# First loads on two DMA queues, in smaller first pieces, and the first norm's squares behind the last input chunk, in a two-layer decoder trunk

## The chip, the cores and the metric

The kernel runs on one core of a Trainium2 chip. The metric is the device time of one execution in microseconds (us). TensorE (PE) multiplies matrices, ScalarE (ACT) and VectorE (DVE) work on rows, GpSimd (POOL) builds masks, and SyncE (SP) issues most DMAs. ScalarE can issue DMAs from its own queue as well. Each engine works through its own queue in order.

## The reference

A sequence of 512 tokens, with 16 learned meta tokens ahead of it, goes through two layers of width 1024. The start of the first layer is what matters here:

```python
h = jnp.concatenate([meta, x], axis=1)
hn = rms_norm(h, norm_mix[0])          # y = x * rsqrt(mean(x*x) + EPS) * g
qkv = hn @ w_qkv                       # 16 heads of 64
h = h + stick_breaking(qkv) @ w_o      # causal, scores q.k
h = h + sq_relu_mlp(rms_norm(h, norm_mlp[0]))
# layer 1: RG-LRU mixer and MLP; then a last rms_norm
```

## The kernel before

The activations stand with features on the partitions: eight chunks of 128 features by 544 columns (the 528 tokens, and the 16 meta tokens a second time). A float32 product is made of three matmuls: every operand is split into a high part and the rest (hi and lo), and hi·hi, hi·lo and lo·hi are summed in PSUM. `split` (L61 to L66) makes the two parts: hi by ScalarE (L63), lo by VectorE (L66). `xs_write` (L143 to L148) does the same for an input chunk, times the gain of the norm, which it reads from the table `vecs`: `xh` (L146) on ScalarE, `xl` (L147) on VectorE. Multiplication by the norm's 1/rms is put off: it is applied where the results leave PSUM.

**The start.** SyncE loads `vecs` (52 KB, L126), and then the loop of L275 to L282 loads, in this order: the first half (four chunks of features) of the first query unit's weights (256 KB, L269), input chunks 0 to 3 (272 KB each, L279), the first half of the first key unit, the second query half, chunks 4 to 7, the second key half. Every piece is split as soon as it has landed. `act.preload_act_table_set` (L273) loads ScalarE's table of functions ahead of it all.

**The first products.** 96 matmuls (tiles `z` as outputs) make the first query and key unit from these pieces. `v_load` then loads two pieces of value weights and splits them to `vhi` and `vlo`; these two tiles take the two buffers of the tag "hs", which hold input chunks 0 to 3 and 4 to 7 until everything that reads these chunks is done, the squares of the norm among them. Four windows of values of 24 matmuls each (`pvs`, tiles `g`) follow; a fifth window needs the PSUM buffer of the first two, which `v_out` (L414, L415) gives back.

**The first norm.** `Norm.add` squares a chunk on ScalarE (`acc` L166 for chunk 0, `sq` L169 for the others) and adds it into `acc` on VectorE (L170). There is one buffer `sq`, so square and sum alternate. The eight calls stand behind the first value window in the program, in a block of priority raised by HP // 4 = 100. `first_norm` sums `acc` over the features by matmuls (tiles `o`), takes the root (L84) and the reciprocals (L177, L343). Only then are queries and keys scaled and written (`qk_out`, `put_q`, `put_k`), the values written (`v_out`), and only then the score matmuls of the first head pair start (tiles `z` in `do_z`, which begin with `ident` times a mask). Behind them come eight head pairs of attention, whose query and key products of the next pair fill TensorE, then the MLPs and the recurrent layer.

**What sets the order.** The program is planned ahead: each engine's queue is filled with the instruction of the smallest place in the program, less its raised priority, among those whose operands are there by the plan. `after(ins, earlier)` keeps an instruction behind others of the same engine in that order; it adds no wait between engines.

Of the kernel before, what the change touches and what calls it, by code (L numbers as in the profile page):

```python
# [18 lines left out]
AF = mybir.ActivationFunctionType  # L19
ALU = mybir.AluOpType  # L20
PSUM = bass.MemoryType.PSUM

P = 128
KC = 8
# [3 lines left out]
HT = T // 2  # L28
TX = T + NM
# [11 lines left out]
HP = 400  # L41
# [4 lines left out]
def tile_hybrid_trunk(ctx: ExitStack, tc: tile.TileContext, h0, vec, wqk, wv, wo,  # L46
                      win, wrg, wig, wout, wup, wdn, out):
    nc = tc.nc
    act, dve, pool, pe = nc.scalar, nc.vector, nc.gpsimd, nc.tensor
# [8 lines left out]
    def f32(ap):  # L58
        return ap.bitcast(F32)

    def split(src, hi, lo, hi_eng=None, lo_eng=None):  # L61
        if hi_eng is None or hi_eng is act:
            act.activation(out=hi, in_=src, func=AF.Copy)  # L63
        else:
            hi_eng.tensor_copy(out=hi, in_=src)
        (lo_eng or dve).tensor_tensor(out=lo, in0=src, in1=f32(hi), op=ALU.subtract)  # L66
# [4 lines left out]
    def after(ins, earlier):  # L71
        for i in earlier:
            tc.add_manual_dep(ins.ins, i.ins.name,
                              mybir.DependencyInfo(mybir.DependencyClass.NoSync, mybir.DependencyReason.DATA),
                              reason="table set order")

    def table(out, in_, func, tset, **kw):
        if runs["set"] != tset:
            runs["before"], runs["now"], runs["set"] = runs["now"], [], tset
            if tset == "natural_log_exp_and_others":  # L80
# [8 lines left out]
    LNEXP, EXP, SIG, SQRT, GELU = ("natural_log_exp_and_others", "exp_and_others", "sigmoid_and_others",  # L89
                                   "sqrt_and_others", "gelu_apprx_tanh_and_others")  # L90
# [32 lines left out]
                mm(outs[i], wlo, cut(xhi, i), False, last and j == n - 1)  # L123

    vecs = const.tile([P, NV], F32, name="vecs")
    nc.sync.dma_start(out=vecs, in_=vec)  # L126


    def slot(i, dtype, name, w=TX):
        return xsp.tile([P, w], dtype, tag=f"x{i}", name=name)  # L130
# [7 lines left out]
    xh = [slot(c, F32R, f"xh{c}") for c in range(KC)]  # L138
    xl = [slot(8 + c, F32R, f"xl{c}") for c in range(KC)]
# [3 lines left out]
    def xs_write(c, h_c, g0, c0=0, c1=T):  # L143
        xh, xl = xs["h"], xs["l"]
        g = vecs[:, g0 + c:g0 + c + 1]
        act.activation(out=xh[c][:, c0:c1], in_=h_c[:, c0:c1], func=AF.Copy, scale=g)  # L146
        dve.scalar_tensor_tensor(out=xl[c][:, c0:c1], in0=h_c[:, c0:c1], scalar=g, in1=f32(xh[c][:, c0:c1]),  # L147
                                 op0=ALU.mult, op1=ALU.subtract)  # L148

    ones = const.tile([P, P], F32, name="ones")  # L150
    dve.memset(ones, -1.0)
# [3 lines left out]
    class Norm:  # L155
# [3 lines left out]
            self.c, self.first = slice(c0, c1), True  # L159
            self.acc = stp.tile([P, TX], F32, tag="acc", name="acc")  # L160

        def add(self, c, h_c, cols=None):
            c = cols or self.c
            if self.first:
                self.first = False
                act.activation(out=self.acc[:, c], in_=h_c[:, c], func=AF.Square)  # L166
            else:
                sq = stp.tile([P, TX], F32, tag="sq", name="sq")
                act.activation(out=sq[:, c], in_=h_c[:, c], func=AF.Square)  # L169
                dve.tensor_tensor(out=self.acc[:, c], in0=self.acc[:, c], in1=sq[:, c], op=ALU.add)  # L170

        def finish(self, ps, cols):
            rstd = stp.tile([P, T], F32, tag="rstd", name="rstd")
# [9 lines left out]
    def h_chunk(c):  # L183
        return hs[c // 4][:, c % 4, :]
# [59 lines left out]
    def attention_layer():  # L244
# [5 lines left out]
        def gtile():  # L250
            return gps.tile([P, S], F32, tag="g", name="g")
# [9 lines left out]
        for m in (0, KC):  # L261
            raw = wp.tile([P, KC * P], F32, tag="raw", name="raw", bufs=3)
            w_first.append((m, raw, wp.tile([P, KC * P], F32R, tag="whi", name="whi"),
                            wp.tile([P, KC * P], F32R, tag="wlo", name="wlo")))

        def first_half(i, a, lo_eng=None):
            m, raw, hi, lo = w_first[i]
            half = slice(a * 4 * P, (a + 1) * 4 * P)
            nc.sync.dma_start(out=raw[:, half], in_=wqk[m][:, half])  # L269
            split(raw[:, half], hi[:, half], lo[:, half], None, lo_eng)  # L270

        nrm = Norm(0, TX)
        act.preload_act_table_set(SQRT)  # L273

        for c in range(KC):  # L275
            if c % 4 == 0:
                hs[c // 4] = hsp.tile([P, 4, TX], F32, tag="hs", name="hs")
                first_half(0, c // 4)
            nc.sync.dma_start(out=h_chunk(c), in_=h0[:, c, :])  # L279
            xs_write(c, h_chunk(c), V_MIX0, 0, TX)  # L280
            if c % 4 == 3:
                first_half(1, c // 4)  # L282

# [120 lines left out]
        def v_mm(pv, w, vhi, vlo):  # L404
            for k in range(KC):
                mm(pv, window(xh[k], w), vhi[:, k, :], k == 0, False)
                mm(pv, window(xl[k], w), vhi[:, k, :], False, False)
                mm(pv, window(xh[k], w), vlo[:, k, :], False, k == KC - 1)
# [158 lines left out]
        for w in range(4):  # L567
            if w % 2 == 0:
                gt = gtile()
            pvs.append(gt[:, 256 * (w % 2):256 * (w % 2) + 256])  # L570
            v_mm(pvs[w], w, *vw)
            if w == 0:
                with tc.high_priority(HP // 4):
                    for c in range(KC):
                        nrm.add(c, h_chunk(c))
        with tc.high_priority(1000):
            first_norm()
        with tc.high_priority(HP):
# [39 lines left out]
        for m in range(KC):  # L618
# [4 lines left out]
            for c0, n in ALL:  # L623
                g = gtile()
# [9 lines left out]
        nrm = Norm()  # L634
# [347 lines left out]
    with ExitStack() as ctx_a:  # L982
        nrm, blocks = attention_layer()
# [17 lines left out]
    nrm, blocks = mixer(nrm1, *xm, gtile)  # L1001
# [118 lines left out]
```

## Time and profile before

| | us |
|---|---|
| median of 3 runs | 1194.46 |
| lowest, highest run | 1193.98, 1195.98 |
| the profiled execution, its own time | 1195.73 |
| its span, first to last instruction | 1194.0 |
| TensorE busy | 1166.0 |

All rows below are of the profiled execution, and their times count from the start of its span; 1.73 us lie around it. A row of a timeline merges equal instructions that follow each other and gives their count as x. A matmul's busy time overlaps with the next one's, so the pace of matmuls is read from counts in a stretch. PEclk is the granted TensorE clock as a share of full speed (1.00 is 2.4 GHz, 0.50 is 1.2 GHz).

### The profile page before, as it was taken

The page shows a single profiled execution, that of the slowest core. Times are in us where ns is not written, and L with a number is a line of the kernel's source. Part 1 is how long each engine was busy: PE and PEld are TensorE (multiplying, and loading weights), DVE is VectorE, ACT ScalarE, POOL GpSimd, SP SyncE. Part 2 cuts the span into 40 slices and gives each one's busy share as a digit, 9 for nine tenths or more (in the row PEclk, how much of TensorE's full clock was granted, in tenths as well). Part 3 has the DMA queues.
Part 4 walks back from the last instruction along what each step waited for, and adds up shares of the span by engine and source line. Part 5 has one row for each costly group of instructions (what it writes and reads, how often), then busy time and mean ns, then how long its engine had stood idle before and what let it go on. Part 6 is the DMA issues. An engine that isn't in the chain of part 4 may idle for free.

```text
span 1194.0 us, 20446 instructions
## 1 busy us (share of the span) xinstructions
PE 1166.0 (98%) x8366; PEld 1104.4 (92%) x8366; DVE 875.5 (73%) x1517; ACT 641.3 (54%) x1063; POOL 4.8 (0%) x24
## 2 busy tenths in 40 slices
PE   7999999999899999999999999999999999999997
PEld 7999999999899999999999999878988988988986
DVE  7887778997895585585586677788975865856854
ACT  6776788776673244243244448757642443533542
POOL 1000000000000000000000000000000000000000
PEclk9999999999999999999999999999999999999999
DMA  6321212041122322322322422223323223223322
GB/s 222 102 74 59 85 37 91 19 145 53 57 93 76 113 91 87 110 92 91 109 93 85 130 72 71 73 86 106 102 76 118 95 96 117 90 88 127 103 71 71
DMA packets 33068, 109.69 MB, mean 92 GB/s; under 512 B 3792, under 2 KB 5840, under 8 KB 32976
## 3 DMA queue, kind: packets, MB, share of 16 engines
q1 hardware_dynamic: 32432, 107.87, 27.9%
q8 instruction: 65, 1.06, 0.4%
q10 hardware_dynamic: 544, 0.52, 0.1%
q14 instruction: 27, 0.22, 0.1%
HBM read 101.96 MB, written 2.10 MB: 87 GB/s over the span
## 4 chain that ended last, share of the span: by engine, by line
PE 87%; DVE 7%; ACT 3%; issue 1%; DMA 1%; SPq 0%; DVEq 0%; ACTq 0%
PE g L103 77%; PE z L103 8%; PE o L103 2%; ACT whi L63 1%; DVE wlo L66 1%; DVE acc L170 1%; DVE th L924 0%; DVE xt L66 0%; DVE xl L147 0%; ACT L84 0%; DVE th L961 0%; DMA hs<-in_h_dram 0%; DVE yl L66 0%; DMA raw<-in_wqk_dram 0%; DMA raw<-in_wup_dram 0%
## 5 line engine op out<-in xcount | busy, mean ns | idle before, releaser
L63 ACT ACTIVATE whi<-raw 128x1024 fp32r<-128x1024 f32 (+1 forms) x150 | 155.8, 1044 | 244.8 <-PE g L103 230.0
L103 PE MATMUL g<-hh,whi 128*128 128x264 f32 (+2 forms) x784 | 231.9, 319 | 3.6 <-ACT whi L63 3.5
L103 PE MATMUL g<-hl,whi 128*128 128x264 f32 (+2 forms) x784 | 231.9, 317 | 0.0
L66 DVE TENSOR_TENSOR wlo<-raw,whi 128x1024 fp32r<-128x1024 f32 (+1 forms) x150 | 180.3, 1207 | 23.5 <-ACT whi L63 23.3
L103 PE MATMUL g<-xt,o 128*128 128x256 f32 (+1 forms) x896 | 163.9, 282 | 0.0
L103 PEld LDWEIGHTS g<-hh,whi 128*128 128x128 f32 x784 | 147.6, 189 | 16.6 <-ACT whi L63 6.4
L103 PEld LDWEIGHTS g<-hl,whi 128*128 128x128 f32 x784 | 147.5, 188 | 9.5
L103 PE MATMUL g<-hh,wlo 128*128 128x264 f32 (+2 forms) x784 | 156.1, 318 | 0.0
L103 PEld LDWEIGHTS g<-xt,o 128*128 128x128 f32 x896 | 137.8, 188 | 0.4
L103 PEld LDWEIGHTS g<-hh,wlo 128*128 128x128 f32 x784 | 120.5, 188 | 10.1
L785 DVE TENSOR_TENSOR hs<-g,hs 128x528 f32<-128x528 f32 (+1 forms) x62 | 42.5, 696 | 113.8 <-PE g L103 113.6
L103 PE MATMUL g<-xb,whi 128*128 128x264 f32 (+1 forms) x352 | 65.2, 286 | 3.4 <-DVE u L725 1.9
L103 PE MATMUL g<-xm,whi 128*128 128x264 f32 (+1 forms) x384 | 67.0, 321 | 0.0
L103 PE MATMUL g<-xt,o1l 128*128 128x256 f32 (+1 forms) x224 | 63.3, 283 | 0.0
L84 ACT ACTIVATE sp<-sp 128x272 f32<-128x272 f32 (+3 forms) x128 | 62.4, 511 | 1.6
L103 PE MATMUL g<-xt,o2l 128*128 128x256 f32 (+1 forms) x224 | 62.2, 282 | 0.0
L103 PEld LDWEIGHTS g<-xm,whi 128*128 128x128 f32 x384 | 56.6, 188 | 5.3
L103 PE MATMUL g<-xh,whi 128*128 128x264 f32 x224 | 59.3, 287 | 0.5 <-DVE v L415 0.5
L103 PE MATMUL g<-xl,whi 128*128 128x264 f32 x224 | 59.2, 287 | 0.0
L747 ACT ACTIVATE hh<-t 128x512 fp32r<-128x512 f32 (+1 forms) x56 | 34.8, 632 | 45.1 <-DVE t L738 45.1
L103 PEld LDWEIGHTS g<-xb,whi 128*128 128x128 f32 x352 | 53.3, 188 | 5.0 <-DVE u L725 3.0
L103 PE MATMUL g<-xa,whi 128*128 128x264 f32 (+1 forms) x288 | 52.3, 282 | 0.0
(244 smaller groups left out, 2730.7 us busy)
## 6 DMA issues: line engine op xcount, KB each, us to landing
raw<-in_wup_dram SPq DMA_DIRECT2D x64, 512.0 KB, 3.5
raw<-in_wdn_dram SPq DMA_DIRECT2D x64, 512.0 KB, 3.5
raw<-in_win_dram SPq DMA_DIRECT2D x16, 512.0 KB, 3.4
raw<-in_wqk_dram SPq DMA_DIRECT2D x14, 512.0 KB, 3.6
q<-q SPq DMA_DIRECT2D x16, 264.0 KB, 4.5
raw<-in_wv_dram SPq DMA_DIRECT2D x8, 512.0 KB, 3.5
raw<-in_wo_dram SPq DMA_DIRECT2D x8, 512.0 KB, 3.7
raw<-in_wout_dram SPq DMA_DIRECT2D x8, 512.0 KB, 3.4
```

The costliest lines, as they stand in the source:

```text
L63: act.activation(out=hi, in_=src, func=AF.Copy)
L66: (lo_eng or dve).tensor_tensor(out=lo, in0=src, in1=f32(hi), op=ALU.subtract)
L84: ins = act.activation(out=out, in_=in_, func=func, **kw)
L103: return pe.matmul(out=o, lhsT=lhsT, rhs=rhs, start=start, stop=stop, skip_group_check=True)
L170: dve.tensor_tensor(out=self.acc[:, c], in0=self.acc[:, c], in1=sq[:, c], op=ALU.add)
L747: act.activation(out=h_, in_=x, func=AF.Square)
L785: dve.tensor_tensor(out=h3, in0=g[:, 0:nb, 0:cw], in1=h3, op=ALU.add)
```

## The change

`vecs` and the first half of the first query unit are issued by ScalarE's queue instead of SyncE's; that half comes in two pieces (one chunk of features, 64 KB, and three, 192 KB), each split by itself. Input chunk 0 comes in two pieces of columns (264 and 280), each with its own `xh` and `xl`. The table load stands behind the first half's instructions in the program. `xs_write` returns its two instructions, and the ones of the last call are handed to `Norm.add`, which keeps the first square (ScalarE) and every sum (VectorE) behind them; the raised priority of the squares is gone. An argument that nothing used (`lo_eng`) falls away.

```diff
--- before.py
+++ after.py
@@ -123,7 +123,7 @@
                 mm(outs[i], wlo, cut(xhi, i), False, last and j == n - 1)
 
     vecs = const.tile([P, NV], F32, name="vecs")
-    nc.sync.dma_start(out=vecs, in_=vec)
+    act.dma_start(out=vecs, in_=vec)
 
 
     def slot(i, dtype, name, w=TX):
@@ -143,9 +143,10 @@
     def xs_write(c, h_c, g0, c0=0, c1=T):
         xh, xl = xs["h"], xs["l"]
         g = vecs[:, g0 + c:g0 + c + 1]
-        act.activation(out=xh[c][:, c0:c1], in_=h_c[:, c0:c1], func=AF.Copy, scale=g)
-        dve.scalar_tensor_tensor(out=xl[c][:, c0:c1], in0=h_c[:, c0:c1], scalar=g, in1=f32(xh[c][:, c0:c1]),
-                                 op0=ALU.mult, op1=ALU.subtract)
+        i = act.activation(out=xh[c][:, c0:c1], in_=h_c[:, c0:c1], func=AF.Copy, scale=g)
+        j = dve.scalar_tensor_tensor(out=xl[c][:, c0:c1], in0=h_c[:, c0:c1], scalar=g, in1=f32(xh[c][:, c0:c1]),
+                                     op0=ALU.mult, op1=ALU.subtract)
+        return [i], [j]
 
     ones = const.tile([P, P], F32, name="ones")
     dve.memset(ones, -1.0)
@@ -159,15 +160,15 @@
             self.c, self.first = slice(c0, c1), True
             self.acc = stp.tile([P, TX], F32, tag="acc", name="acc")
 
-        def add(self, c, h_c, cols=None):
+        def add(self, c, h_c, cols=None, behind=((), ())):
             c = cols or self.c
             if self.first:
                 self.first = False
-                act.activation(out=self.acc[:, c], in_=h_c[:, c], func=AF.Square)
+                after(act.activation(out=self.acc[:, c], in_=h_c[:, c], func=AF.Square), behind[0])
             else:
                 sq = stp.tile([P, TX], F32, tag="sq", name="sq")
                 act.activation(out=sq[:, c], in_=h_c[:, c], func=AF.Square)
-                dve.tensor_tensor(out=self.acc[:, c], in0=self.acc[:, c], in1=sq[:, c], op=ALU.add)
+                after(dve.tensor_tensor(out=self.acc[:, c], in0=self.acc[:, c], in1=sq[:, c], op=ALU.add), behind[1])
 
         def finish(self, ps, cols):
             rstd = stp.tile([P, T], F32, tag="rstd", name="rstd")
@@ -263,21 +264,23 @@
             w_first.append((m, raw, wp.tile([P, KC * P], F32R, tag="whi", name="whi"),
                             wp.tile([P, KC * P], F32R, tag="wlo", name="wlo")))
 
-        def first_half(i, a, lo_eng=None):
+        def first_half(i, a, q=nc.sync, pieces=(0, 4)):
             m, raw, hi, lo = w_first[i]
-            half = slice(a * 4 * P, (a + 1) * 4 * P)
-            nc.sync.dma_start(out=raw[:, half], in_=wqk[m][:, half])
-            split(raw[:, half], hi[:, half], lo[:, half], None, lo_eng)
+            for k0, k1 in zip(pieces, pieces[1:]):
+                x = slice((a * 4 + k0) * P, (a * 4 + k1) * P)
+                q.dma_start(out=raw[:, x], in_=wqk[m][:, x])
+                split(raw[:, x], hi[:, x], lo[:, x])
 
         nrm = Norm(0, TX)
-        act.preload_act_table_set(SQRT)
-
         for c in range(KC):
             if c % 4 == 0:
                 hs[c // 4] = hsp.tile([P, 4, TX], F32, tag="hs", name="hs")
-                first_half(0, c // 4)
-            nc.sync.dma_start(out=h_chunk(c), in_=h0[:, c, :])
-            xs_write(c, h_chunk(c), V_MIX0, 0, TX)
+                first_half(0, c // 4, nc.sync if c else act, (0, 4) if c else (0, 1, 4))
+            if c == 0:
+                act.preload_act_table_set(SQRT)
+            for c0, c1 in ((0, HT), (HT, TX)) if c == 0 else ((0, TX),):
+                nc.sync.dma_start(out=h_chunk(c)[:, c0:c1], in_=h0[:, c, c0:c1])
+                written = xs_write(c, h_chunk(c), V_MIX0, c0, c1)
             if c % 4 == 3:
                 first_half(1, c // 4)
 
@@ -570,9 +573,8 @@
             pvs.append(gt[:, 256 * (w % 2):256 * (w % 2) + 256])
             v_mm(pvs[w], w, *vw)
             if w == 0:
-                with tc.high_priority(HP // 4):
-                    for c in range(KC):
-                        nrm.add(c, h_chunk(c))
+                for c in range(KC):
+                    nrm.add(c, h_chunk(c), None, written)
         with tc.high_priority(1000):
             first_norm()
         with tc.high_priority(HP):
```

## Rows read from the trace of the kernel before

**Rows 1.** Page part 1: busy time, share of the span, instructions, by engine.
```profile
PE 1166.0 (98%) x8366; PEld 1104.4 (92%) x8366; DVE 875.5 (73%) x1517; ACT 641.3 (54%) x1063; POOL 4.8 (0%) x24
```

**Rows 2.** Waits, 0 to 60 us: engine, line, releaser, total us, times, longest.
```profile
PE z L103 <- ACT xh L146: 6.3, 1, 6.3
...
PE o L103 <- DVE acc L170: 1.0, 1, 1.0
```

**Rows 3.** Timeline of SyncE's queue: start us, duration us, line, operation, count.
```profile
0.80 0.39 SPq L126 DMA_DIRECT2D vecs<-in_vec_dram  x1
...
1.72 1.85 SPq L279 DMA_DIRECT2D hs<-in_h_dram  x4
...
5.53 1.12 SPq L279 DMA_DIRECT2D hs<-in_h_dram  x2
```

**Rows 4.** DMA view of single issues: KB each, us from issue to landing.
```profile
vecs<-in_vec_dram SPq DMA_DIRECT2D x1, 52.0 KB, 1.9
...
raw<-in_wqk_dram SPq DMA_DIRECT2D x1, 256.0 KB, 3.0
...
hs<-in_h_dram SPq DMA_DIRECT2D x2, 272.0 KB, 6.2
```

**Rows 5.** Source view of line 1053: ns of an issue, min/median/max.
```profile
L1053 ACTq DMA_DIRECT2D out_dram<-hg x2: 378/400/423, 1189.1 to 1190.4; - x2
```

**Rows 6.** Timeline of ScalarE, 0 to 33 us (in brackets idle before, and its releaser).
```profile
0.80 1.28 ACT L273 ACT_TABLE_LOAD   x1 [0.80 <-PEq L1101]
...
13.22 0.74 ACT L146 ACTIVATE xh<-hs,vecs 128x544 fp32r<-128x544 f32 x1
...
14.39 1.05 ACT L63 ACTIVATE vhi<-raw 128x1024 fp32r<-128x1024 f32 x1
...
18.66 0.66 ACT L169 ACTIVATE sq<-hs 128x544 f32<-128x544 f32 x1 [0.79 <-DVE acc L170]
...
32.42 0.37 ACT L414 ACTIVATE v<-g,rtok 128x128 fp32r<-128x128 f32 x1
```

**Rows 7.** Timeline of VectorE, 14 to 28 us.
```profile
14.13 0.72 DVE L170 TENSOR_TENSOR acc<-acc,sq 128x544 f32<-128x544 f32 x1
14.76 0.78 DVE L147 SCALAR_TENSOR_TENSOR xl<-hs,vecs,xh 128x544 fp32r<-128x544 f32 x1
15.46 0.69 DVE L66 TENSOR_TENSOR wlo<-raw,whi 128x512 fp32r<-128x512 f32 x1
...
17.90 0.73 DVE L170 TENSOR_TENSOR acc<-acc,sq 128x544 f32<-128x544 f32 x1 [1.11 <-ACT sq L169]
19.35 0.73 DVE L170 TENSOR_TENSOR acc<-acc,sq 128x544 f32<-128x544 f32 x1 [0.72 <-ACT sq L169]
...
22.16 0.72 DVE L170 TENSOR_TENSOR acc<-acc,sq 128x544 f32<-128x544 f32 x1
22.80 2.35 DVE L66 TENSOR_TENSOR vlo<-raw,vhi 128x1024 fp32r<-128x1024 f32 x2
...
27.03 1.16 DVE L66 TENSOR_TENSOR wlo<-raw,whi 128x1024 fp32r<-128x1024 f32 x1
```

**Rows 8.** Chain that ended last, in order of time: start us, us, what.
```profile
22.93 1.83 PE o L103 x12
...
38.09 2.86 PE g L103 x24
```

**Rows 9.** Timeline of TensorE at the first score matmuls.
```profile
35.96 0.70 PE L103 MATMUL z<-m,ident 128*128 128x320 f32 x4
```

**Rows 10.** Stretches: length, busy us (count) of PE, PEld, DVE, ACT, POOL; PEclk, DMA, GB/s.
```profile
11.00:12.00 1.00, 1.00 (x6) 1.00 (x6) 1.00 (x2) 1.00 (x2) 0.00 (x0) 1.00 1.05 409
13.00:14.00 1.00, 1.00 (x11) 1.00 (x10) 1.00 (x2) 1.00 (x3) 0.00 (x0) 1.00 0.83 225
303.00:306.00 3.00, 0.92 (x5) 0.64 (x5) 2.30 (x7) 1.98 (x5) 0.00 (x0) 0.92 0.00 0
306.00:309.00 3.00, 3.00 (x15) 3.00 (x15) 1.88 (x5) 0.69 (x2) 0.00 (x0) 0.51 0.02 5
```

## The prediction

> **What bounds the kernel now.** Read the page's busy shares first: TensorE is busy for 98% of the span [rows 1], so a change can only return time in which TensorE stood still or ran at half its pace. The change touches nothing behind the first norm, so the waits of the first 60 us are read next. TensorE waits twice there for more than half a microsecond: 6.3 us for the first input part `xh`, and 1.0 us for the norm's sum `acc` [rows 2]. A third loss is no wait. In the stretch from 11 to 12 us TensorE does 6 matmuls, from 13 to 14 us it does 11, with the same operands and busy throughout [rows 10]. The clock column shows 1.00 in both, but 5 to 6 matmuls a microsecond is the pace of 306 to 309 us, 15 in 3 us, where the column shows 0.51, so the first matmuls seem to run at the lower of the two clock levels.
>
> From 12 us on TensorE has work until the score matmuls start at 35.96 [rows 9]. Those need queries and keys, and so the norm: its last sum on VectorE ends at 22.16 + 0.72 = 22.88 [rows 7], its matmuls start at 22.93 [rows 8], and roots, reciprocals, scaling, splitting and the copies of the queries fill the 35.96 - 22.88 = 13.1 us behind it. TensorE reaches the scores just as they become ready. **So two chains meet at 35.96**, TensorE's work and the chain through `acc`, and a gain needs both to be earlier.
>
> **The start (two queues, smaller pieces).** SyncE spends 0.80 to 1.72 on `vecs` and the first weights before it issues chunk 0 [rows 3]. Afterwards its first issue is 132 KB of chunk 0, at 0.80. ScalarE issues three DMAs at 0.38 to 0.42 us each [rows 5], from 0.80 to 2.0, and what is queued behind them is its table load of 1.28 us [rows 6], until 3.3. A first load lands 1.9 us (52 KB) to 3.0 us (256 KB) after its issue [rows 4]; so the 64 KB of weights, issued at 1.2, land at 3.1 to 4.2 and chunk 0's first piece at 2.7 to 3.8. Splitting the 128 columns and writing 264 columns of `xh` is an estimate of 0.3 + 0.4 us, from 0.74 us for 544 [rows 6]. The first matmul starts at 4.0 to 4.9; I take 4.2, since 64 KB is near the 52 KB row. Against 6.3 that is 2.1 us, bounds 1.4 to 2.3. The smaller pieces add three ScalarE and three VectorE instructions or halves of them; they lie in time in which both engines wait for loads, and cost nothing.
>
> The rows show chunk 0's first issue 0.92 us behind the first one [rows 3]. The Trainium skill ("DMA: Bandwidth & Descriptors", section "Issuing engines are not separate DMA queues") says that issuing from several engines saves only the time of issuing, since all transfers share the same 16 DMA engines. By that rule alone the start would gain 0.9 us instead of 2.1; the forecast would stay, since it is set by the other chain, and the first rival would give 1192.6.
>
> **TensorE's own work** therefore reaches the scores at 35.96 - 2.1 - 1.0 = 32.9, if the wait for `acc` disappears from its queue.
>
> **The squares (the part that decides).** Before, three of the seven sums lie ahead of the last `xl`: the third starts at 14.13, the last `xl` at 14.76 [rows 7]. They filled gaps there. Afterwards all seven come behind it. What the last `xl` gains: chunk 7 is issued at about 6.2 (the second of the two issues from 5.53 to 6.65 [rows 3]) and lands 6.2 us later [rows 4], at 12.4; the loads are queued 6 us deep, so an earlier start moves this by little. With 0.74 us for `xh` [rows 6] and 0.78 for `xl` [rows 7] the last `xl` ends at 13.9 instead of 15.54. The split of the last key weights stands behind it, 0.6 us from start to start (15.46 to 16.06), so the first sum starts at 14.5. Square and sum alternate through one buffer: sums at 17.90 and 19.35 [rows 7] with the square at 18.66 between them [rows 6] give 1.45 us a round. The seventh sum starts at 14.5 + 6 x 1.45 = 23.2 and ends at 23.9.
>
> Other work queues into the rounds. `vhi` needs the buffer that chunks 0 to 3 hold until their squares are done, so its two splits (1.05 us each [rows 6]) now fall between squares, and the next pair's weight split does too. Each is longer than the 0.73 us of a sum beside which it can hide, by 0.3 us: three cost 1.0, bounds 0 to 1.0. `acc` is then ready at **24.9** (bounds 23.9 and, next paragraph, 27.3) instead of 22.88: the hold costs the chain 2.0 us.
>
> `vlo` needs chunks 4 to 7 released, so it becomes ready together with the last sum, at the end of the last square. Before, the sum went first and `vlo` took 2.35 us behind it [rows 7]. The squares now lose their raised priority, and `vlo` stands ahead of them in the program; if the planner puts it first, `acc` is late by another 2.35 us, at 27.3. No row shows that order, so its cost lies between 0 and 2.35; I take 0, as in the row, and keep 2.35 for the range.
>
> Behind `acc` the chain gets shorter by one step: the split at 27.03 (1.16 us, 1.1 from start to start) stood between the reciprocals [rows 7]. Its load waits for a buffer that comes free earlier now, and I count it done before: minus 1.1, bounds 0 and 1.1. The scores start at 24.9 + 13.1 - 1.1 = 36.9, which is **0.9 us later** than 35.96.
>
> **The clock.** TensorE comes at 32.9 and stands until 36.9, 4 us. From 303 to 306 us it was busy for only 0.92 us, the granted clock fell, and 306 to 309 ran at 0.51 [rows 10]. Lost: 3 x 0.08 + 3 x 0.49 = 1.7 us. I charge these 1.7 us to the first scores, bounds 0 (if the score chain and not TensorE sets the pace there) and 1.7.
>
> **Sum.** +0.9 + 1.7 = +2.6 against the profiled execution: 1195.7 + 2.6 = 1198.3. The median of the runs lies 1.3 lower, so the forecast is 1194.5 + 2.6 = **1197.1**. All of the start's 2.1 us and the 1.0 us turn into waiting at the scores. Other parts (the `after` calls, the returned instructions) add no instruction.
>
> **Rivals.**
> - *TensorE's gap gets filled, and the start's gain stays.* The fifth value window (24 matmuls, 2.86 us, now at 38.09 behind the first scores [rows 8]) can move into the gap if `v_out` frees its buffer early. For it: values of the first windows wait for the roots alone, and ScalarE has gaps there. Against it: `v_out` starts only at 32.42 [rows 6], 9.5 us behind `acc`, behind all of the queries' work. Then 32.9 + 2.86 = 35.8 is when TensorE asks for scores; with `acc` at 23.9 these are ready at 35.9, nothing falls to the lower clock, and the gain is 2.1 + 1.0 = 3.1: 1191.4.
> - *The two ends cancel.* `acc` at 23.9 to 24.9 and the gap short or partly filled, no clock loss: -1 to +1, about 1194.5. For it speaks that both chains met within a few tenths before.
> - *`vlo` ahead of the last sum.* From the sum above, +2.35: +4.9, 1199.4. It decides if the split of `vlo` stands ahead of the last L170 in VectorE's order.
> - *The change doesn't do what it says.* ScalarE's three issues and the table load hold its first split so long that the start gains nothing (4.9 or later, and `vecs` late): then the hold alone is left, and the time is that of the second rival or of the sum, 1194.5 to 1197.
>
> **How the numbers follow.** Some 0.2% (2.4 us) is what a measurement of this kernel tells from no change: below 1192.1 is faster, above 1196.9 slower. Forecast (sum, `vlo` behind) 0.33, half of it over that bound; `vlo` ahead 0.25, all slower; filled gap 0.22, all faster; ends cancel 0.17 and start without gain 0.03, within. That is faster 0.22, same 0.37, slower 0.41. The range holds both rivals at its ends: 1191.2 to 1199.5; the forecast's own range, with all its bounds (0 to 1.0 for the three splits, 0 to 1.1 for the step that leaves the chain, 0 to 1.7 for the clock), is 1194.4 to 1198.2.
>
> **What would show it.** First matmul near 4.2 and no wait of TensorE for `acc`; the last `xl` near 13.9; seven sums at 1.45 us or more a round behind it; the last sum's end near 24.9 (27.3 with `vlo` ahead); a new wait of TensorE at the first scores or at the fifth window, some 4 us, and 0.50 in the clock column behind it. The forecast is wrong if `acc` is ready before 23 us, if the squares run ahead of chunk 7 after all, or if the fifth window or the next pair's products stand ahead of the scores and TensorE has no gap between 30 and 40 us.

## The result, and the profile after

| | kernel before | changed kernel |
|---|---|---|
| time, median of 6 runs each | 1196.09 us (1193.98 to 1197.49) | 1202.39 us (1199.72 to 1204.38) |
| ratio, 95% interval | | 1.0053 [1.0041, 1.0066] |
| profiled execution, its span | 1195.7, 1194.0 | 1204.11, 1202.4 |

The change makes the kernel slower by 6.3 us, on the forecast's side of no change, but 5.3 us above the forecast and outside its range (1191.2 to 1199.5). Of these 5.3 us, 1.6 are the starting point: the forecast added its +2.6 to the median of three runs, 1194.5, and over six runs that median is 1196.1. The change itself came out 3.7 us above the forecast, +6.3 instead of +2.6. The six runs after carry mean granted clocks from 0.997 and 0.996 (1200.05 and 1199.72) down to 0.992 (1204.38); the profiled one, 0.993, is among the longer ones. So the profile has 8.4 us to explain, the medians 6.3.

**Waits.** Waits of TensorE, 0 to 60 us, as in [rows 2] (line, releaser: total us, times, longest):

```profile
PE z L103 <- ACT whi L63: 7.6, 2, 5.0
PE g L103 <- DVE vlo L66: 3.3, 1, 3.3
PE z L103 <- DMA q<-q: 1.7, 2, 1.5
```

The wait for `acc` is gone, as forecast. The first wait, 6.3 us before, became two that make 7.6, and two waits are new: for `vlo`, which the value matmuls need, and for the copies of the queries, just before the first scores.

**The start.** ScalarE after, then DMA issues of 0 to 14 us (KB each, us from issue to landing), against [rows 3 to 6]:

```profile
0.80 0.41 ACTq L126 DMA_DIRECT2D vecs<-in_vec_dram  x1
1.24 0.94 ACTq L271 DMA_DIRECT2D raw<-in_wqk_dram  x2
2.21 1.28 ACT L280 ACT_TABLE_LOAD   x1 [2.21 <-issue]
...
4.68 0.31 ACT L63 ACTIVATE whi<-raw 128x128 fp32r<-128x128 f32 x1 [0.65 <-DMA raw<-in_wqk_dram]
...
7.47 0.75 ACT L146 ACTIVATE xh<-hs,vecs 128x544 fp32r<-128x544 f32 x1 [2.07 <-DMA hs<-in_h_dram]
8.13 0.64 ACT L170 ACTIVATE sq<-hs 128x544 f32<-128x544 f32 x1
8.67 0.51 ACT L63 ACTIVATE whi<-raw 128x384 fp32r<-128x384 f32 x1
```

```profile
hs<-in_h_dram SPq DMA_DIRECT2D x7, 272.0 KB, 5.9
...
raw<-in_wqk_dram ACTq DMA_DIRECT2D x1, 192.0 KB, 5.9
...
raw<-in_wqk_dram ACTq DMA_DIRECT2D x1, 64.0 KB, 3.4
vecs<-in_vec_dram ACTq DMA_DIRECT2D x1, 52.0 KB, 2.6
```

The 64 KB piece lands at 1.24 + 3.4 = 4.6. The 192 KB behind it need 5.9 us, where 256 KB in one piece needed 3.0 before [rows 4], and their split waits in ScalarE's queue behind chunk 1 and a square, until 8.67. TensorE does its first matmuls and stands again (below, the idle time before 9.23). An early first piece brought the first few matmuls forward and left the other products later.

**VectorE behind the last `xl`**, against [rows 7]:

```profile
15.24 0.72 DVE L171 TENSOR_TENSOR acc<-acc,sq 128x544 f32<-128x544 f32 x1
...
16.68 0.73 DVE L171 TENSOR_TENSOR acc<-acc,sq 128x544 f32<-128x544 f32 x1
18.13 0.72 DVE L171 TENSOR_TENSOR acc<-acc,sq 128x544 f32<-128x544 f32 x1 [0.72 <-ACT sq L170]
20.72 0.73 DVE L171 TENSOR_TENSOR acc<-acc,sq 128x544 f32<-128x544 f32 x1 [1.86 <-ACT sq L170]
...
24.25 0.72 DVE L171 TENSOR_TENSOR acc<-acc,sq 128x544 f32<-128x544 f32 x1 [0.72 <-ACT sq L170]
25.70 2.36 DVE L66 TENSOR_TENSOR vlo<-raw,vhi 128x1024 fp32r<-128x1024 f32 x2 [0.72 <-ACT sq L170]
27.98 0.72 DVE L171 TENSOR_TENSOR acc<-acc,sq 128x544 f32<-128x544 f32 x1
```

Seven sums, all behind the last `xl` (end 15.32), 1.45 us apart where nothing comes between. `vlo` stands ahead of the last sum.

**TensorE**, with the idle time in brackets, against [rows 8, 9]:

```profile
9.23 0.59 PE L103 MATMUL z<-xh,whi 128*128 128x264 f32 x1 [2.56 <-ACT whi L63]
...
26.98 0.39 PE L103 MATMUL g<-vlo,xh 128*128 128x256 f32 x1 [3.31 <-DVE vlo L66]
...
31.68 1.17 PE L103 MATMUL o<-ones,acc 128*128 128x1 f32 x10
...
41.50 0.70 PE L103 MATMUL z<-m,ident 128*128 128x320 f32 x4
43.73 0.95 PE L103 MATMUL z<-q,k 128*128 128x256 f32 x6 [1.53 <-DMA q<-q]
```

The norm's matmuls, which followed the last sum at once before (22.88 and 22.93), start 3.0 us after it (28.70 and 31.68). They wait for nothing by then: they stand in TensorE's queue behind 26 value matmuls which came with `vlo` at 26.98.

**Stretches**, columns as in [rows 10]: two at the lower pace behind the waits, and the long stretch after the first minute.

```profile
28.00:31.00 3.00, 3.00 (x17) 3.00 (x16) 1.83 (x3) 0.00 (x0) 0.00 (x0) 0.54 0.86 266
...
46.00:48.00 2.00, 2.00 (x11) 2.00 (x11) 1.27 (x4) 2.00 (x8) 0.00 (x0) 0.50 0.01 4
...
60.00:300.00 240.00, 240.00 (x1842) 235.99 (x1842) 202.39 (x489) 187.01 (x405) 0.00 (x0) 1.00 0.24 74
```

From 60 to 300 us TensorE has next to no gap: it is busy for 240.00 of these 240 us after the change, for 239.93 before, and for at least 239.4 in each run below. What it loses ahead of 60 us can't be caught up there, and this gives a way of **keeping account**: a kernel's span is longer by TensorE's additional idle time in the first 60 us, plus half of the additional time in which it was busy at the lower of its two clock levels (1.2 instead of 2.4 GHz). The idle time comes from one row per kernel, the stretch from 0 to 60 us (before, after):

```profile
0.00:60.00 60.00, 52.13 (x392) 50.70 (x393) 45.94 (x88) 44.22 (x87) 4.83 (x24) 1.00 0.51 162
```

```profile
0.00:60.00 60.00, 47.06 (x323) 45.47 (x324) 38.64 (x74) 35.79 (x70) 5.10 (x24) 0.94 0.42 136
```

Idle: 60 - 52.13 = 7.9 before, 12.9 after, **+5.1**. Lower clock: the trace records the granted clock's steps. It rises for the first time at 11.99 before and 14.59 after (busy till then 5.6 and 7.0 us), and after it falls to 0.5 for 3.41 us at 28.24 and again at 45.31; both kernels have one more stretch of 3.41 us near 305 to 315. That is half of 1.4 + 6.8, **+4.1**. The sum, 9.2, stands beside 8.4 measured. "TensorE: Matmul & The Clock Gate" in the Trainium skill, section "Terms", prices throttled time in the same way, time times one minus the granted share. These kernels agree with it for the part of that time in which TensorE is busy: e5, below, has 10.2 us at 0.5 ahead of 60 us and works in 6.1 of them; its sum is 8.0 with the busy part and 10.1 with all of it, and its span differs by 8.2.

The account describes where the time went, and is no proof of a cause. It leaves out TensorE's idle time behind 60 us, which is 20.1 us before and 19.9 to 21.3 us in the others; with it, sum and span would lie up to 1.5 us apart (e10).

### The profile page after: what moved, and what is told of

It reads as the page before. It is cut to its first block, busy times and chain, and to the rows that moved or that the text cites. A ratio compares the mean times of both kernels' runs of the same rounds, so it can differ in the third digit from the quotient of the medians.

```text
span 1202.4 us, 20456 instructions
## 1 busy us (share of the span) xinstructions
PE 1169.5 (97%) x8366; PEld 1108.0 (92%) x8366; DVE 876.1 (73%) x1519; ACT 642.4 (53%) x1065; POOL 5.1 (0%) x24
## 4 chain that ended last, share of the span: by engine, by line
PE 88%; DVE 6%; ACT 4%; issue 1%; DMA 1%; SPq 0%; DVEq 0%; ACTq 0%
PE g L103 79%; PE z L103 8%; PE o L103 2%; ACT whi L63 1%; DVE wlo L66 1%; DMA hs<-in_h_dram 0%; DVE rstd L178 0%; DVE acc L171 0%; DVE th L926 0%; DVE th L963 0%; DVE yl L66 0%; DMA q<-q 0%; ACT r L84 0%; ACT sq L170 0%; DVE hg L1054 0%
## 5 line engine op out<-in xcount | busy, mean ns | idle before, releaser
L63 ACT ACTIVATE whi<-raw 128x1024 fp32r<-128x1024 f32 (+2 forms) x151 | 155.9, 1039 | 248.4 <-PE g L103 235.9
L66 DVE TENSOR_TENSOR wlo<-raw,whi 128x1024 fp32r<-128x1024 f32 (+2 forms) x151 | 180.5, 1201 | 21.9 <-ACT whi L63 21.6
L103 PEld LDWEIGHTS g<-hh,wlo 128*128 128x128 f32 x784 | 120.4, 188 | 10.1
L84 ACT ACTIVATE sp<-sp 128x288 f32<-128x288 f32 (+3 forms) x128 | 62.3, 508 | 1.8
L63 ACT ACTIVATE o<-raw 128x1024 fp32r<-128x1024 f32 x28 | 29.7, 1062 | 42.5 <-DVE raw L690 35.6
```

Of the source, the lines that this page charges most:

```text
L84: ins = act.activation(out=out, in_=in_, func=func, **kw)
L103: return pe.matmul(out=o, lhsT=lhsT, rhs=rhs, start=start, stop=stop, skip_group_check=True)
```

## The experiments

All accounts in one table; each is told below. "At 0.5" is the time in which TensorE was busy at the lower clock after the first rise, ahead of 60 us, and the length of the late stretch behind it. "Sum" is idle + half of (until the first rise + at 0.5, both parts), against the kernel before; "span" is what the same two profiled executions differ by.

| run | median (before beside it) | ratio [95%] | idle 0 to 60 | busy until first rise | at 0.5 before 60, behind | sum | span |
|---|---|---|---|---|---|---|---|
| before | | | 7.9 | 5.6 | 0, 3.4 | | |
| after | 1202.39 (1196.09) | 1.0053 [1.0041, 1.0066] | 12.9 | 7.0 | 6.8, 3.4 | +9.2 | +8.4 |
| e1_loads_only | 1197.99 (1196.39) | 1.0013 [1.0003, 1.0022] | 8.9 | 5.5 | 3.4, 3.4 | +2.7 | +2.0 |
| e2_hold_only | 1203.13 (1196.39) | 1.0060 [1.0044, 1.0077] | 12.9 | 6.3 | 3.2, 3.4 | +7.0 | +7.3 |
| e3_hold_prio | 1200.74 (1196.39) | 1.0039 [1.0024, 1.0054] | 10.3 | 7.6 | 3.4, 0 | +3.4 | +3.8 |
| e4_no_prio | 1199.51 (1196.39) | 1.0025 [1.0015, 1.0036] | 10.3 | 6.3 | 6.8, 0 | +4.5 | +4.0 |
| e5_after_spare | 1205.26 (1195.68) | 1.0079 [1.0064, 1.0094] | 14.9 | 4.9 | 6.1, 0 | +8.0 | +8.2 |
| e7_vecs_on_act | 1195.55 (1195.68) | 0.9998 [0.9988, 1.0007] | 7.6 | 5.1 | 3.4, 0 | -0.5 | -0.4 |
| e8_warm | 1197.91 (1195.68) | 1.0016 [1.0006, 1.0025] | 4.7 | 3.5 | 9.9, 3.4 | +0.7 | +3.0 |
| e9_sq3 | 1193.70 (1195.68) | 0.9984 [0.9974, 0.9993] | 6.6 | 5.8 | 0, 0 | -2.9 | -2.7 |
| e10_after_sq3 | 1200.34 (1196.27) | 1.0040 [1.0025, 1.0055] | 11.6 | 6.0 | 6.4, 0 | +5.5 | +4.7 |
| e13_sq3_vec | 1194.90 (1196.27) | 0.9989 [0.9979, 0.9998] | 7.3 | 5.1 | 0, 3.4 | -0.8 | -0.7 |
| e14_loads_sq3 | 1195.22 (1196.27) | 0.9990 [0.9980, 0.9999] | 7.9 | 7.4 | 0, 0 | -0.8 | -1.2 |
| e15_loads_whole | 1197.57 (1196.27) | 1.0009 [1.0000, 1.0018] | 9.3 | 5.7 | 3.4, 0 | +1.5 | +1.0 |

Sum and span differ by 0.8 us at most, but for e8: its added matmuls, 3.7 us at the lower clock, are work of 1.9 us at the higher, and with them its sum is 2.6 beside 3.0. Each profile is of one execution; the mean granted clock differs between executions of one kernel (0.994 to 0.998 over the runs of the kernel before), so a stretch at 0.5 in one profile need not stand in the next execution, and the medians average over them.

### The three parts apart

The change has three parts: other loads, the hold, and the raised priority that was taken from the squares. Four combinations.

e1, the changed kernel with the squares as before:

```diff
-                for c in range(KC):
-                    nrm.add(c, h_chunk(c), None, written)
+                with tc.high_priority(HP // 4):
+                    for c in range(KC):
+                        nrm.add(c, h_chunk(c))
```

> The new loads (ScalarE's queue, smaller first pieces) with the squares as before: raised priority, nothing held. Theory PRIORITY (the lost raise puts the split of vlo and TensorE's value matmuls ahead of the norm) and theory HOLD (seven sums behind the last chunk) both expect the loads to cost only what TensorE's first 96 matmuls lost in the changed kernel (23.05 against 21.29 us, 1.8 us) or less: 0 to +2 us against the kernel before. Theory LOADS (the pieces that share the DMA engines starve TensorE and everything behind it) expects most of the loss, +4 to +6 us. First matmul near 5.0, then a wait of some 2.5 us for the second piece of weights under all three.

e2, the kernel before with the hold (`xs_write` and `Norm.add` as in the change) and without the priority:

```diff
-            xs_write(c, h_chunk(c), V_MIX0, 0, TX)
+            written = xs_write(c, h_chunk(c), V_MIX0, 0, TX)
...
-                with tc.high_priority(HP // 4):
-                    for c in range(KC):
-                        nrm.add(c, h_chunk(c))
+                for c in range(KC):
+                    nrm.add(c, h_chunk(c), None, written)
```

> The loads as before, the squares held behind the last chunk and without raised priority. PRIORITY and HOLD expect +4 to +6 us: last sum ends near 28, behind vlo, and TensorE waits about 3 us for vlo and then about 1.5 us at the first scores. LOADS expects 0 to +1 us.

e3, the changed kernel with the hold and the priority given back:

```diff
-                for c in range(KC):
-                    nrm.add(c, h_chunk(c), None, written)
+                with tc.high_priority(HP // 4):
+                    for c in range(KC):
+                        nrm.add(c, h_chunk(c), None, written)
```

> The changed kernel with the raised priority given back to the squares, still held behind the last chunk; the last sum then stands ahead of vlo on VectorE. PRIORITY expects most of the loss gone: 0 to +2.5 us against the kernel before, last sum's end near 26.3 instead of 28.7. HOLD expects the loss to stay, +4 to +6 us. LOADS expects +4 to +6 us.

e4, the kernel before without the priority and nothing else:

```diff
-                with tc.high_priority(HP // 4):
-                    for c in range(KC):
-                        nrm.add(c, h_chunk(c))
+                for c in range(KC):
+                    nrm.add(c, h_chunk(c))
```

> The kernel before with one edit: the raised priority of the squares is taken away, nothing is held, loads as before. VectorE's order then has vlo (2.35 us) ahead of the last sum. PRIORITY expects +2.5 to +5 us: last sum's end near 25.2 instead of 22.9, TensorE waiting for vlo. HOLD and LOADS expect -0.5 to +1 us.

Measured against the kernel before: loads +1.6, lost priority +3.1, hold and lost priority +6.7, loads and hold +4.3, all three +6.3. The loads are not the main cause: on top of the other two they change nothing (6.3 beside 6.7). The hold costs 2.7 (e3 less e1) to 3.6 (e2 less e4), the lost priority 3.1 alone and 2.0 beside loads and hold; of these four differences the last is the only one whose two intervals overlap (1.0041 to 1.0066, and 1.0024 to 1.0054). The hold by itself, with the old loads and the priority kept, was not run.

No theory held in all four. PRIORITY was right on e4 and too low on e3 (4.3 instead of 0 to 2.5), HOLD was right on e3 and wrong on e4 (3.1 instead of at most 1), LOADS was wrong on e1, e2 and e4. Hold and lost priority each cost time on top of the rest.

What the priority did is one place in VectorE's order; e3 with its first matmuls of the norm, then e4:

```profile
25.35 0.72 DVE L171 TENSOR_TENSOR acc<-acc,sq 128x544 f32<-128x544 f32 x1 [0.72 <-ACT sq L170]
25.99 2.35 DVE L66 TENSOR_TENSOR vlo<-raw,vhi 128x1024 fp32r<-128x1024 f32 x2
...
26.13 1.05 PE L103 MATMUL o<-ones,acc 128*128 128x1 f32 x8 [2.50 <-DVE acc L171]
```

```profile
22.20 2.35 DVE L66 TENSOR_TENSOR vlo<-raw,vhi 128x1024 fp32r<-128x1024 f32 x2
24.47 0.72 DVE L170 TENSOR_TENSOR acc<-acc,sq 128x544 f32<-128x544 f32 x1
```

With the priority the last sum goes ahead of `vlo`, held or not; without it `vlo` goes first, held or not. So the removed priority, not the hold, put `vlo` ahead. The place of the norm goes with it: in e1 and e3, as before, the norm's matmuls start 0.05 us behind the sum; in e4 and e2 they start 2.4 and 3.1 us behind it, behind value matmuls, as in the changed kernel.

### The buffers that couple `vlo` to the squares

e5: the changed kernel, with `vhi` and `vlo` of the first value load in buffers that no square keeps.

```diff
-            vhi = hsp.tile([P, KC, 256], F32R, tag="hs", name="vhi")
-            vlo = hsp.tile([P, KC, 256], F32R, tag="hs", name="vlo")
+            p_, t1, t2 = (hsp, "hs", "hs") if g else (vqp, "q", "v2")
+            vhi = p_.tile([P, KC, 256], F32R, tag=t1, name="vhi")
+            vlo = p_.tile([P, KC, 256], F32R, tag=t2, name="vlo")
```

> The changed kernel, with one thing different: the first vhi and vlo go into two buffers that are free by then and no longer into the two buffers that the input chunks leave. In the changed kernel vlo's split can't start before the last square has read its chunk (25.70), the value matmuls behind it start at 26.98 and the norm's matmuls stand behind them in TensorE's queue, 3.0 us after the sum is ready (28.70 to 31.68). COUPLED: the hold costs time because the squares that it moves keep vlo's buffers taken. Then the value matmuls start by about 23, right behind the 96 products, the norm's matmuls at about 28.7 to 29.0 (the sums take as long as before), the first scores at about 41, and the time falls by about 2.5 from the 1202.4 of the changed kernel, to 1199 to 1200.5. SUM ALONE: what costs is only the 13.4 us from the last xl to the last sum; the value matmuls merely fill TensorE's wait, the norm still comes first at 31 and the time stays at 1201.5 to 1203.

Both expectations missed the time. The wait for `vlo` is gone and the value matmuls start at 21.77, as the first one had it; the norm still comes at about 31, as the second one had it; and the kernel is no faster than the changed one: by the medians it is some 3 us slower (1.0079 [1.0064, 1.0094] and 1.0053 [1.0041, 1.0066], intervals that just touch). The waits of TensorE, and the norm's first matmuls:

```profile
PE z L103 <- ACT whi L63: 7.3, 2, 4.5
PE z L103 <- DVE qk L366: 3.8, 2, 2.1
PE z L103 <- DMA q<-q: 3.8, 1, 3.8
```

```profile
30.68 1.17 PE L103 MATMUL o<-ones,acc 128*128 128x1 f32 x10
```

The sum is ready at 27.70, and the norm again starts 3.0 us behind it, after value matmuls without a gap. These are the work with which TensorE covers the norm's chain up to the scores. Done ahead of the norm, they leave it standing behind it, for 7.6 us. The counts of all runs with `vlo` ahead of the sum fit this. Of the 96 value matmuls, 92 stand between the norm and the first q·k matmuls in the kernel before, in e1 and in e3, and TensorE waits for no copies of queries there; 66 stand there in the changed kernel (wait 1.7 us), 64 in e2 (1.9), 58 in e4 (2.3), 43 in e10, below (4.4), and 21 here (7.6 in all). So e5 and e10, which lose the wait for `vlo`, wait for longer at the scores.

### The chain of sums

e9: the kernel before, with three buffers for the first norm's squares instead of one.

```diff
...
-                sq = stp.tile([P, TX], F32, tag="sq", name="sq")
+                sq = pair(c0 % 3, [P, TX], F32, "sq") if self.many else stp.tile([P, TX], F32, tag="sq", name="sq")
...
-        nrm = Norm(0, TX)
+        nrm = Norm(0, TX, True)
```

> The kernel before, with three buffers for the first norm's squares instead of one, so that a square doesn't wait until VectorE has read the one before it. This shortens the chain of sums, which all my accounts of the loss turn on, in the kernel where it is nearly hidden. CHAIN COUNTS: the last sum ends by about 18 to 19 instead of 22.9, the wait of 1.0 in front of the norm's matmuls is gone, these start behind the 96 products at about 21.5 to 22, recip and scores 1 us earlier, time 1195.0 to 1195.6. HIDDEN: VectorE's and ScalarE's earlier squares push back the splits that the value matmuls need, TensorE waits there instead, and the time is 1196 to 1197. WORSE: earlier squares push xh or the second weights' whi back on ScalarE, the 96 products end later than 21.2 and the time is above 1197.

Two rows of VectorE, and the first of the norm on TensorE:

```profile
17.70 0.71 DVE L170 TENSOR_TENSOR acc<-acc,sq 128x544 f32<-128x544 f32 x1
18.34 2.34 DVE L66 TENSOR_TENSOR vlo<-raw,vhi 128x1024 fp32r<-128x1024 f32 x2
```

```profile
20.96 1.17 PE L103 MATMUL o<-ones,acc 128*128 128x1 f32 x10
```

The sum is ready at 18.41 instead of 22.88, and the norm starts at 20.96 instead of 22.93. TensorE waits for nothing but its first operands and once for 0.4 us. The earlier squares do push the last `xl` back (end 17.18 instead of 15.54) and with it the last of the 96 products (23.01 instead of 21.16), as the third expectation feared, but the norm's matmuls now stand ahead of these. This kernel is **faster than both**: 1193.70, ratio 0.9984 [0.9974, 0.9993], and below what the first expectation gave it (1195.0 to 1195.6). The first 60 us give -1.2 of the account (idle -1.3, clock +0.1); the rest of the profile's -2.7 is the late stretch, which this execution does not have. Of the 2.0 us in the medians only about 1.2 is therefore traced to the sums.

e10: the same three buffers in the changed kernel, the hold in place.

> The changed kernel, the hold in place, with three buffers for the first norm's squares instead of one. The sums no longer take 1.45 us each; they are ready at 24 to 25.5 instead of 28.7. In this kernel's order of work the norm's matmuls stand behind 53 value matmuls on TensorE (23 in the changed kernel from the end of its wait on). SUM: if the time goes with the moment at which the sum is ready, the norm's matmuls start at about 25, the scores at 37 to 38, and the time is 1197 to 1198.5. PLACE IN THE QUEUE: if it goes with where the norm's matmuls stand among TensorE's instructions, they start at 29 to 31 although the sum is ready 4 to 6 us earlier, and the time stays at 1201 to 1204.

The sum is ready at 25.13, 3.6 us earlier than in the changed kernel. The norm's matmuls start at 28.29, 3.2 us behind it, since 53 value matmuls stand ahead of them (30 in the changed kernel, 26 of these behind its wait, not 23 as the expectation has it); that is 3.4 us earlier than in the changed kernel, and the scores are 3.0 us earlier (40.71 and 43.73). TensorE's idle time falls by 1.3 us only: the wait for `vlo` is gone, but with its cover used up ahead of the norm TensorE waits 4.4 us for the queries' copies. The time lies between the two expectations; the gain on the changed kernel, some 2 us by the medians, is not settled by the intervals, which overlap (1.0040 and 1.0053). In e3 the norm starts two microseconds earlier still, at 26.13, right behind its sum and ahead of all but four value matmuls, and its time is the same as e10's (1.0039). So an early norm alone does not decide either. The place of the norm in TensorE's queue was not changed by itself, and its own price stays open.

### The loads

e7: the kernel before, with `vecs` alone on ScalarE's queue. e15: the loads of the change, the first weights in one piece of 256 KB and chunk 0 whole, squares as before.

```diff
-    nc.sync.dma_start(out=vecs, in_=vec)
+    act.dma_start(out=vecs, in_=vec)
```

> The kernel before, with only the table of vectors issued by ScalarE's queue; the first weights stay whole on SP's. START GAINS: with one issue fewer ahead of the weights on SP's queue the first product starts at about 5.5 instead of 6.3 and everything behind moves by as much: 1195.4 to 1196.0 beside 1196.4. SMALL PIECE IS THE FAULT: the loss of the loads alone (1.6 us) sat in the 192 KB piece and the chunk behind it (landing at 7.6 and 7.4), so that without the piece the 96 products end no later than 21.2 and the time is not above 1196.5. TABLE IS THE FAULT: ScalarE's issue and its load of functions, now behind each other, delay xh, and the time is again 1197.5 to 1198.5.

```diff
-                first_half(0, c // 4, nc.sync if c else act, (0, 4) if c else (0, 1, 4))
+                first_half(0, c // 4, nc.sync if c else act)
...
-            for c0, c1 in ((0, HT), (HT, TX)) if c == 0 else ((0, TX),):
+            for c0, c1 in ((0, TX),):
...
```

> The table and the first weights issued by ScalarE's queue as in the changed kernel, but the weights in one piece of 256 KB and the first chunk whole; the squares not held, with their raised priority. PIECES ARE THE FAULT: the late 192 KB piece is what made the loads cost 1.6 us; with one piece again the whole lands at about 5 and the time is 1195.4 to 1196.2 beside 1195.7 to 1196.4. QUEUE IS THE FAULT: weights and chunks on two queues at once share the transfer engines in any size; the weights land at 6 or later, the 96 products end past 21.4 and the time is 1197 to 1198.5.

e7 starts at 5.74 instead of 6.31 and gains nothing that can be measured. Its norm starts 0.6 us earlier too (22.33), behind a wait of 1.1 us for `acc`; but the stretch at 0.5 that follows at 24.85 brings its first score matmuls to 36.93, 1.0 us later than before. e15 is not measurably better than e1 (1.0009 [1.0000, 1.0018] and 1.0013 [1.0003, 1.0022]): its time, 1197.57, is that of the second expectation, and nothing shows that the small piece is the fault. Its weights land at 1.25 + 4.2 = 5.4, the first split stands behind two `xh` and two squares in ScalarE's queue and starts at 6.33, the first matmul at 7.00:

```profile
4.50 1.38 ACT L146 ACTIVATE xh<-hs,vecs 128x544 fp32r<-128x544 f32 x2
5.79 0.64 ACT L170 ACTIVATE sq<-hs 128x544 f32<-128x544 f32 x1
6.33 0.61 ACT L63 ACTIVATE whi<-raw 128x512 fp32r<-128x512 f32 x1
```

So the weights land later than before, and ScalarE's order has their split behind work that it preceded before; the two were not tried apart.

e14: all of the change's loads, squares as before, three buffers. e13: three buffers and `vecs` on ScalarE's queue, the edits of e9 and e7 together.

> All of the changed kernel's loads, the squares not held and with their raised priority, and three buffers for the squares. LOADS COST BY THEMSELVES: the second piece and the chunk behind it land late (7.6 and 7.4) whatever becomes of the sums, the 96 products end at 22 to 23.5, and the time is 1.0 to 2.0 above that of three buffers alone, 1194.7 to 1195.7 beside 1195.7. LOADS COST ONLY THROUGH THE SUMS: in the run with the loads alone the sum was ready 1.0 later than before (23.91 and 22.88), and the norm waited 1.7 for it; without that wait the loads are free or gain, and the time is 1193 to 1194.

> The kernel before, with three buffers for the squares (alone 1193.70 beside 1195.68, recip at 24.00) and the table of vectors issued by ScalarE's queue (alone 1195.55 beside 1195.68, first product at 5.74). CHAIN: in the run with the table alone the earlier start was lost at the norm; with the sums ready early the 96 products decide, and 0.3 to 0.6 us of the earlier start arrive: 1192.9 to 1193.4 beside 1195.7. NO GAIN: the earlier products only bring the first higher clock forward and not the norm: 1193.5 to 1194.2.

e14 is 1.0 us below the kernel before (0.9990 [0.9980, 0.9999]). Three buffers alone gave 2.0 (e9), so beside them the loads still cost about 0.9, where they cost 1.6 with one buffer. That is nearer to the first expectation, that the loads cost by themselves; by the medians only the rest, some 0.7, came through the sum (for which e1 waits 1.7 us), and the intervals don't settle it. e13 gains 1.4 (0.9989 [0.9979, 0.9998]) and no more than e9: the earlier start brings nothing that can be measured even where the sums are early.

### An early clock

e8: the kernel before, with eight matmuls of constants ahead of the first product.

```diff
+NW = 8
...
+        wt = ops.tile([P, S], F32, tag="o0", name="o0")
+        with tc.high_priority(HP):
+            for _ in range(NW):
+                mm(wt[:, 0:P], ones, ones, True, True)
```

> The kernel before, with eight 128x128 matmuls of constants put ahead of the first product; their result is not used. TensorE then works from about 2 us on and its clock should rise before 11.99. TWO CHAINS: the norm waits for the sum of squares (1.0 us of TensorE's wait already in the kernel before), so that products ended earlier only lengthen that wait: the sum stays ready at 22.9, scores at 36.3 to 36.5, time 1196 to 1197 (or worse, 1198, if the longer wait brings a stretch at half clock of its own, as behind the longer waits of the runs so far). PRODUCTS BOUND: the 96 products' end sets the rest; it moves from 21.2 to 17 to 19, scores by 2 or more, time 1194 to 1194.5.

```profile
1.12 3.72 PE L104 MATMUL o<-ones 128*128 128x128 f32 x16 [1.12 <-DVE eps L154]
```

```profile
8.00:14.00 6.00, 5.65 (x24) 5.35 (x25) 6.00 (x10) 5.89 (x10) 0.00 (x0) 0.50 1.02 378
```

The clock rises at 4.64, while TensorE works on constants; between 4.84 and 8.9 it waits and works by turns, the clock falls at 8.05 and comes back at 14.88, later than the 11.99 without the constants. The kernel is slower by 2.2 us, at 1197.91. The first expectation had 1198 in brackets, for a stretch at 0.5 behind a longer wait at the norm. There is a stretch, at 25.12, but the wait is as long as before (1.0 us); the sum is ready at 24.11, and the last product starts at 22.65 instead of 21.16. That the raised clock would be lost again while the operands come in was not foreseen.

## Why the prediction was wrong, step by step

- **The start, 4.2 instead of 6.3, gain 2.1.** First matmul at 5.04, just outside the bounds of 4.0 to 4.9, and a second wait of 2.56 us behind it; the 96 products end 1.8 us later than before (last one 22.92, before 21.16), part of it since the clock rises at 14.59 and not at 11.99. The step failed because it followed the first piece alone: the row of 256 KB in 3.0 us was taken for a queue of its own, and the 192 KB and chunk 1 beside it were not priced. They took 5.9 and 5.7 us. "DMA: Bandwidth & Descriptors" in the Trainium skill, section "Issuing engines are not separate DMA queues", was the better guide: e7, which moves an issue and nothing else, gains 0.57 us at the first product, within the 0.9 that its rule left. With hold and lost priority beside it the mistake counted little, since the forecast had that gain end in waiting anyway, and e2 with the old start is as slow as the changed kernel; alone, the loads cost 1.6 (e1).
- **`acc` no longer waited for.** Right for TensorE's record, and beside the point: the wait moved to `vlo` (3.3 us), which the hold delays in the same way.
- **Last `xl` at 13.9.** 15.32. Chunk 7 lands at about 12.8, near the estimate of 12.4, by luck: it is issued at 7.8 instead of 6.2 and needs 5.0 us instead of 6.2. But the four last `xl` stand one behind the other on VectorE until 15.32, 0.7 us each. Term mis-sized by 1.4.
- **Rounds of 1.45 and three splits.** 16.68 to 18.13 is 1.45. The first sum starts at 15.24, six rounds make 8.7, `vlo` 2.28 from start to start, and the last sum starts at 27.98: the splits took 27.98 - 15.24 - 8.7 - 2.28 = 1.8 instead of 1.0. That is made up elsewhere: in e3, with `vlo` behind, the last `xl` ends at 14.97 and the sum at 26.08: 11.1 us, where 24.9 - 13.9 = 11.0 were forecast.
- **`vlo` ahead of the last sum, taken at 0.** This is the step that failed. It puts the last sum back by 2.3 us, from `vlo`'s start to the sum's, in the changed kernel, in e2 and in e4, and by 0 in e1 and e3. The text named the reason, the squares' lost priority and `vlo`'s place ahead of them in the program, and then took the row of before, which was planned with the priority. With it and the late `xl`, 24.9 + 1.4 + 2.35 is 28.65; measured 28.70. In time the lost priority costs 3.1 us alone (e4, 1.0025 [1.0015, 1.0036]) and, by the medians, 2.0 of the changed kernel's 6.3. It is not all of the miss: with the order that the forecast took, e3 is still 4.3 above the kernel before, where +2.6 was forecast. The 1.7 that are left lie in terms which e3 has as well, the late first products, the late `xl` and the clock; no run tells these apart.
- **The norm right behind `acc`.** Not thought of as a step at all. On TensorE the 26 value matmuls that `vlo` releases stand ahead of the norm, 16 of them in the stretch at the lower clock from 28.24 on, and it starts 3.0 us late. This hangs on the same order: where the sum goes ahead of `vlo` and one buffer holds the squares, the norm starts less than 0.1 us behind its sum. From the norm's start to the first q·k matmuls it was 36.50 - 22.93 = 13.6 before and is 43.73 - 31.68 = 12.05: 1.5 shorter, where 1.1 were forecast for the step that leaves the chain.
- **A gap of 4 us at the scores.** There are two, 3.3 at `vlo` and 1.7 at the scores, 5.0 together. With the start's +1.3 and the 1.0 that went, the waits add 5.3, near the +5.1 of idle time; the forecast had 4 - 2.1 - 1.0 = +0.9.
- **The clock, 1.7.** +4.1 in the profiled execution: two stretches, and a later first rise.
- **Rivals.** `vlo` ahead of the last sum happened and was priced at 1199.4, without the late `xl`, the queue and the second stretch. The start without gain happened too, and worse than its bound of 4.9; in the text it had 3 chances in 100.

What stays open: why one gap is followed by a stretch at the lower clock and another is not. The kernel before waits 1.01 us at 21.9 without one, e7 waits 1.1 us and has one at 24.85.

## What to carry to other kernels

Where TensorE has no gap later on, add up its idle time and half its time at the lower clock over the stretch that the change touches: here this gave every span within a microsecond (for e8 with its added matmuls counted as work), while a forecast along one chain had to be right about each place in each queue. A priority that is removed is a change of order at each place where two things become ready together, so look at what stands beside the instructions in the program, and do not take the order from the profile made with the priority. And if a chain of small steps alternates through a single buffer, try more buffers: here three gained 2.0 us by the medians (e9), where moving the same steps behind the last chunk without their priority lost 6.7 (e2).

## What the runs showed that was not expected

- A first load split over two queues landed later: 192 KB took 5.9 us behind 64 KB, 256 KB on ScalarE's queue beside chunks on SyncE's took 4.2, and 256 KB on SyncE's alone 3.0 [rows 4].
- The granted clock can rise and fall again before the kernel is under way (e8: up 4.64, down 8.05, up 14.88).
- In the first microseconds the clock column shows 1.00 at half pace: 7 matmuls from 13 to 14 us in the changed kernel, with TensorE busy throughout, where the kernel before, its clock up since 11.99, does 11 [rows 10].
